# A gated feed-forward block in fp32: seven block products for the first matmul in place of a plain one, and one level instead of two for the second

## Chip, cores and metric

The kernel runs on one core of a Trainium2 chip. The metric is the device time of one execution in microseconds, on the slowest (here the only) core; three runs of the kernel before gave 2157.34, 2160.28 and 2160.47 us. All inputs and outputs are float32.

## The reference

One layer of a decoder: 512 tokens, width 2048. The first half (modulation vectors, an input projection, windowed attention, sparse attention with top-k keys, an output projection) is untouched in its arithmetic. What matters here is the second half:

```python
D_MODEL = 2048; SEQ = 512; D_FF = 5632
def conv_ffn(h, w_up, conv_w, conv_b, w_down):
    u, g = jnp.split(h @ w_up, 2, axis=-1)
    u = causal_depthwise_conv_width_3(u, conv_w) + conv_b
    return (jax.nn.silu(u) * g) @ w_down
...
h = rms_norm(x, norm_ffn[l]) * (1.0 + sc2) + sh2
x = x + g2 * conv_ffn(h, w_up[l], conv_w[l], conv_b[l], w_down[l])
return rms_norm(x, norm_final)
```

`h @ w_up` is (512 x 2048) by (2048 x 11264): the first product. `(...) @ w_down` is (512 x 5632) by (5632 x 2048): the second.

## The kernel before

**Precision.** TensorE (PE) multiplies in fp32r. Each fp32 operand is cut into a high part (a cast on ScalarE, ACT) and a low part (a subtraction on VectorE, DVE): `split` (L155) and `split_to` (L201). A product is three matmuls, high x high, high x low, low x high (`mm3`, L162).

**Slots.** The program is a list of slots. `drive` (L385) goes through it: for slot i it starts the loads of the slots up to 5 ahead (`AHEAD_LOAD`, L28), the cuts of those up to 3 ahead (`AHEAD_SPLIT`, L30), then the matmuls of slot i, then `step` (L307), which lets every started generator go on by one piece, and the slot's `after`. Modulation vectors for later use are computed alongside, paced by the columns PE has been given (`pace`, L290; `mod_gen`, L245; multiply-adds at L216). Dependences are found from the tiles, and a scheduler orders each engine's instructions; `tc.keep_in_program_order` pins some. SP issues the loads, POOL (GpSimd) issues the stores that accumulate in DRAM, and some loads.

**First product.** Row f of 44 stands for 128 of the 5632 features: a unit u of 16 x 128 weight rows and a unit g. `unit_slots` (L368) makes four slots of each unit, 4 contraction tiles x 3 matmuls per slot, the weights stationary and 512 tokens moving (line L53 in the profile). The normalised activations are held as `h2h`, `h2l`. Row f is 96 matmuls of 512 columns. `conv_gen` (L1031) does the convolution, silu and gate; its result stays in SBUF.

**Second product.** Four rows make a group g. While group g runs through the first product, group g - 1 runs through the second: its slots (`down_products`, L1285) are put between those of the first product. A group's (tokens x features) by (features x outputs) product is cut into 2 x 2 blocks and done with seven block products (Strassen's scheme with Winograd's sums) in place of eight: three plain ones (`Product`, L1152; operand sums in `combos`, L1061) and four that are cut once more into 2 x 2 and done with seven again (`Deep`, L1198; `cut_seven`, L1079). Here the activations are stationary and 512 columns of weights move: 72 matmuls in the plain ones and 84 in the deep ones, where a direct product has 192. Weight sums are made on VectorE (L1168, L1171, L1222, L1225). Results go from PSUM (L1194, L1249, L1252) to DRAM, where POOL accumulates them in `total` (`add_up`, L1143). This is done for the first ten groups.

**Close.** The last group (rows 40 to 43) is multiplied directly with 256 tokens moving (`last_slots`, L1329), in two halves of the tokens, 384 matmuls. `join_gen` (L1295) loads `total` on POOL's queue (L1305), transposes it on PE (`cT`) and adds it to the residual `x2`; the final norm and the output stores follow (`finish_half`, L1376). The residual waits in DRAM (`x2d`) from the start of the feed-forward part.

**Memory.** `ring` holds weights in flight and short-lived pairs; `big` holds two tiles of 4 MB, tags b2 and b3, in turn for h1, the mixed attention output mh/ml, and h2. PSUM has eight banks: acc 2, sc 3, tp 2, o 1.

Of the kernel before, what the change touches and what calls it, by code (L numbers as in the profile page):

```python
# [15 lines left out]
P = 128  # L16
# [17 lines left out]
def hybrid_trunk(ctx, tc, xT, cT, wm, bm, nrm, wik, wiq, wi1, sinks, kvn, wuk, wuv, rel, onehot,  # L34
# [26 lines left out]
    ring = ctx.enter_context(tc.tile_pool(name="ring", bufs=1))  # L61
    big = ctx.enter_context(tc.tile_pool(name="big", bufs=1))
    h1h = big.tile([P, KT, T], F32R, tag="b2", name="h1h")
    h1l = big.tile([P, KT, T], F32R, tag="b3", name="h1l")
# [256 lines left out]
    class Raw:  # L321
        def __init__(self, src, name, pool=None):
            self.src, self.name, self.pool, self.t = src.rearrange("p a b -> p (a b)"), name, pool, {}

        def load(self, part):
            if part not in self.t:
                x, name = self.src[:, 512 * part:512 * part + 512], f"{self.name}_{part}"
                if self.pool in env:
                    env["late"] = n = env.get("late", 0) + 1
                    if n < 7:  # L330
                        t = env[self.pool].tile([P, 512], F32, tag="raw", bufs=6, name=name)
                    else:
                        t = ring.tile([P, 512], F32, tag="raw", bufs=RAW, name=name)
                    self.t[part] = t
                    tc.keep_in_program_order(sp.dma_start(t, x))
                else:
                    self.t[part] = load_raw(x, name)
# [12 lines left out]

    class Kept:

        def __init__(self, raw, part, mm, after=None):
            self.raw, self.part, self.mm, self.after, self.w = raw, part, mm, after, None

        def split(self):
            if self.w is None:
                n, part = self.part
                self.w = env["h2h"][:, n], env["h2l"][:, n]
                if self.raw:  # L360
                    self.load()
                    split_to(*self.w, self.raw.t[part])

        def load(self):
            if self.raw:
                self.raw.load(self.part[1])
# [18 lines left out]
    def drive(slots, lo, hi, halves=False, ahead=AHEAD_LOAD):  # L385
        for i in range(lo, hi):
            for j in range(i, min(i + ahead + 1, len(slots))):
                slots[j].load()
            for j in range(i, min(i + AHEAD_SPLIT + 1, len(slots))):
# [590 lines left out]

    def squares(dt, name):
# [14 lines left out]
    def wo_after(dt):  # L996
        def f(ps):
            xk = env["x2"][dt // 4][:, dt % 4]
            with later(-60 if dt == KT - 1 else 0):
                dve.scalar_tensor_tensor(xk, ps, mcol(2, dt), xk, OP.mult, OP.add)  # L1000
                squares(dt, "sq2_")
        return f
# [8 lines left out]

    acts, ugate = {}, {}
    LEAD = 3
# [6 lines left out]
    def g_after(f):  # L1020
        def g(ps):
            start(conv_gen(f, ugate[f], ps))
        return g

    SG = FT // 4 - 1
    total = [[dram.tile([P, 2, T], F32, name=f"total{h}_{dq}") for dq in range(4)] for h in range(2)]
    x2d = [dram.tile([P, 4, T], F32, name=f"x2d{i}") for i in range(4)]
    pair, cuts, keep3, held = {}, {}, {}, {}
    W = P * 2

    def conv_gen(f, ups, gps):  # L1031
        g, k = divmod(f, 4)
        p, half = k % 2, k // 2
        if half == 0:
            pair[g, p] = env["p2"].tile([P, 2, T], F32, tag="u", bufs=2, name=f"cu{g}_{p}")
        u = pair[g, p][:, half]
        act.activation(u, ups, AF.Identity, bias=cb_sb[:, f:f + 1], scale=cw_sb[:, f, 2:3])
        dve.scalar_tensor_tensor(u[:, 1:], ups[:, :T - 1], cw_sb[:, f, 1:2], u[:, 1:], OP.mult, OP.add)
        dve.scalar_tensor_tensor(u[:, 2:], ups[:, :T - 2], cw_sb[:, f, 0:1], u[:, 2:], OP.mult, OP.add)
        act.activation(u, u, AF.Silu)  # L1040
        dve.tensor_tensor(u, gps, u, OP.mult)
        yield
        if g == SG:
            if "pe" in env:
                last_acts(f)
            else:
                env.setdefault("late", []).append(f)
        elif half:
            yield from combos(g, p)

    def last_acts(f):
        g, k = divmod(f, 4)
        fh = env["pe"].tile([P, T], F32R, tag="fh", bufs=4, name=f"fh{f}")
        fl = env["pe"].tile([P, T], F32R, tag="fl", bufs=4, name=f"fl{f}")
        split_to(fh, fl, pair[g, k % 2][:, k // 2])
        acts[f] = fh, fl


    PLAIN, DEEP, TURNS = (0, 2, 3), (1, 4, 5, 6), (1, 5, 4, 6)

    def combos(g, p):  # L1061


        u = pair[g, p].rearrange("p a b -> p (a b)")
        a11, a21, a12, a22 = [u[:, W * i:W * i + W] for i in range(4)]
        if p == 0:
            cuts[g] = [env["pf"].tile([P, 3, 2, W], F32R, tag=f"a{x}", bufs=1, name=f"a{x}{g}") for x in "hl"]
        ah, al = cuts[g]
        k = keep3[g, p] = env["pf"].tile([P, 4, W], F32, tag="op", bufs=2, name=f"op{g}_{p}")
        split_to(ah[:, 0, p], al[:, 0, p], a11)  # L1070
        act.copy(k[:, 0:2], u[:, 2 * W:].rearrange("p (a b) -> p a b", a=2))
        dve.tensor_tensor(k[:, 2], a21, a22, OP.subtract)
        dve.tensor_tensor(a21, a11, a21, OP.subtract)
        yield
        dve.tensor_tensor(a11, k[:, 2], a11, OP.subtract)
        dve.tensor_tensor(k[:, 3], a12, a11, OP.add)
        split_to(ah[:, 1:3, p], al[:, 1:3, p], u[:, :2 * W].rearrange("p (a b) -> p a b", a=2))

    def cut_seven(g, i):  # L1079


        if (g, i) not in cuts:
            ah, al = cuts[g, i] = [env["pd"].tile([P, 7 * P], F32R, tag=f"b{x}", bufs=2, name=f"b{x}{g}_{i}")
                                   for x in "hl"]
            x0, x1 = [keep3[g, p][:, DEEP.index(i)] for p in range(2)]
            split_to(ah[:, :P], al[:, :P], x0[:, :P])
            split_to(ah[:, P:3 * P], al[:, P:3 * P], x1)
            dve.tensor_tensor(x1[:, P:], x0[:, P:], x1[:, P:], OP.subtract)
            dve.tensor_tensor(x0[:, P:], x0[:, :P], x0[:, P:], OP.subtract)
            dve.tensor_tensor(x0[:, :P], x1[:, P:], x0[:, :P], OP.subtract)  # L1090
            dve.tensor_tensor(x1[:, :P], x1[:, :P], x0[:, :P], OP.add)
            split_to(ah[:, 3 * P:5 * P], al[:, 3 * P:5 * P], x0)
            split_to(ah[:, 5 * P:], al[:, 5 * P:], x1)
        return cuts[g, i]

    class Quads:


        BUFS = {0: 2, 1: 1, 2: 2, 3: 2}

        def __init__(self, g):
            self.g, self.b = g, {}

        def load(self, i, c):
            if (i, c) in self.b:
                return
            tag, at = (0, 3) if i == 6 else (i, i)
            t = env["pa"].tile([P, 2, 512], F32, tag=f"rq{tag}", bufs=self.BUFS[tag], name=f"rq{self.g}_{i}_{c}")
            sp.dma_start(t, wdn[self.g, c + 2 * (at % 2)][:, 2 * (at // 2):2 * (at // 2) + 2])
            self.b[i, c] = t  # L1110

    def cut_w(x, n):
        hi_t = env["pd"].tile([P, 2, 512], F32R, tag="dh", bufs=2, name=f"dh{n}")
        lo_t = env["pd"].tile([P, 2, 512], F32R, tag="dl", bufs=2, name=f"dl{n}")
        k = x.shape[1]
        split_to(hi_t[:, :k], lo_t[:, :k], x)
        return [(hi_t[:, i], lo_t[:, i]) for i in range(k)]


    STEPS = {0: ((0, 1), (), 0, ((0, 1, 0),)),  # L1120
             2: ((2, 3), ((1, 3, 1), (0, 3, 3)), 3, ((3, 2, 3),)),
             3: ((), (), 1, ())}

    BLOCK = {1: 2, 4: 3, 5: 0, 6: 6}

    GOES = {1: ((0, 0),), 4: ((1, 0),), 5: ((0, 2), (1, 2)), 6: ((0, 2),)}

    STEPS2 = [((0, 1), (), 0, ((0, 1, 0),)),
              ((2,), ((1, 3, 1), (0, 3, "t")), "t", (("t", 2, 2),)),
              ((3, 6), (), 1, ()),  # L1130
              ((5, 4), (), 0, ())]
    OPERAND = [0, 1, 3, 4, 2, 6, 5]

    SIGN = [1, 1, -1, -1, 1, -1, -1]
# [6 lines left out]
    begun = set()  # L1141

    def add_up(g, to, x):  # L1143
        if id(to) in begun:
            ins = pool.dma_start(to, x, accum_op=OP.add)  # L1145
        else:
            ins = pool.dma_start(to, x)
            begun.add(id(to))
# [472 lines left out]
```

## Time and profile before

| | |
|---|---|
| runs | 2157.34, 2160.28, 2160.47 us; median 2160.28 |
| span of the profiled execution | 2157.9 us (no separate time is given for it; it lies 2.4 us under the median) |
| mean granted TensorE clock | 0.994 |
| busy: PE, VectorE, ScalarE, POOL | 98%, 78%, 55%, 11% |
| moved by DMA | 428.93 MB, mean 199 GB/s |
| feed-forward part up to its closing stage | from 767.3 to 2086.8 us |
| closing stage and end | from 2086.8 to 2157.9 us |

How to read it: PE's busy share counts pipelined matmuls from start to a modelled end, which overlap; the distance between the starts of two of them is what one costs in a full stream. The line of a matmul is L53, that of the helper, so groups go by the names of tiles: `u18ps<-h2h,u18r_2h` is row 18's u unit; `p`, `p_0s` to `p_6s` are plain and deep blocks of the second product (`dh`, `dl` their cut weights, `ah`, `bh` cut activations); `d_0ps` to `d_3ps` the closing stage.

### The profile page before, as it was taken

The numbers are of one execution on the slowest core, as the hardware profiler recorded it, in microseconds if no ns is written. First come the engines' busy times: TensorE is split into PE (matmuls) and PEld (weight loads), VectorE is DVE, ScalarE is ACT, GpSimd is POOL, SyncE is SP. The second block draws the span as 40 slices with busy tenths as digits, with TensorE's granted clock in tenths as the row PEclk, the third lists the DMA queues.
The fourth block names the chain that finished last, engine by engine and source line by source line (L and its number), as shares of the span: only waits on it lengthen the run. The fifth ranks groups of instructions, "written<-read, shape, count | busy, mean of one in ns | idle before, by whom it ended". The sixth has DMA issues, their size and how long they took to land.

```text
span 2157.9 us, 29881 instructions
## 1 busy us (share of the span) xinstructions
PE 2116.7 (98%) x10264; PEld 1721.8 (80%) x10264; DVE 1692.4 (78%) x3005; ACT 1187.4 (55%) x2222; POOL 244.0 (11%) x356
## 2 busy tenths in 40 slices
PE   8999999899999999999999999999999999999997
PEld 4777877787788878888888888888888888888887
DVE  2887899778777775788888878787787877787876
ACT  4324886777722273555555555555555555555554
POOL 0000000111033200101011010111101110111110
PEclk9999999999999999999999999999999999999998
DMA  9783221676598644688888897988778787877772
GB/s 388 266 288 107 58 68 59 198 213 207 174 366 286 228 155 139 199 225 201 221 190 214 219 223 199 223 208 204 189 186 192 193 181 209 174 196 176 168 265 98
DMA packets 160840, 428.93 MB, mean 199 GB/s; under 512 B 18479, under 2 KB 25663, under 8 KB 154544
## 3 DMA queue, kind: packets, MB, share of 16 engines
q1 hardware_dynamic: 118128, 277.09, 38.2%
q0 software_dynamic: 41696, 148.36, 32.4%
q8 instruction: 80, 1.31, 0.2%
q10 hardware_dynamic: 864, 1.57, 0.2%
q14 instruction: 72, 0.59, 0.1%
HBM read 323.41 MB, written 103.55 MB: 198 GB/s over the span
## 4 chain that ended last, share of the span: by engine, by line
PE 85%; DVE 5%; ACT 4%; issue 3%; DMA 2%; POOL 0%; SPq 0%; DVEq 0%; POOLq 0%; ACTq 0%
PE p L53 8%; PE p_0s L53 5%; PE qip L53 4%; PE p_5s L53 1%; PE p_6s L53 1%; PE p_1s L53 1%; PE o L53 1%; PE ckv L53 1%; PE mrow L53 1%; PE scb L53 1%; DVE wk L699 1%; PE mps L53 1%; DVE top L696 1%; DMA ct<-total 1%; DMA mraw<-in_wm_dram 1%
## 5 line engine op out<-in xcount | busy, mean ns | idle before, releaser
L216 DVE SCALAR_TENSOR_TENSOR macc<-mraw,cact,macc 128x512 f32<-128x512 f32 x240 | 179.4, 748 | 12.3 <-DMA mraw<-in_wm_dram 10.3
L203 DVE TENSOR_TENSOR dl<-rq,dh 128x1024 fp32r<-128x1024 f32 x60 | 73.4, 1223 | 45.2 <-ACT dh L202 40.3
L53 PE MATMUL p<-dl,ah 128*128 128x512 f32 x240 | 94.6, 394 | 0.0
L203 DVE TENSOR_TENSOR dl_0s<-rq,dh_0s 128x1024 fp32r<-128x1024 f32 x40 | 49.0, 1226 | 58.0 <-ACT dh_0s L202 57.8
L53 PE MATMUL p<-dh,ah 128*128 128x512 f32 x240 | 94.2, 392 | 0.0
L53 PE MATMUL p<-dh,al 128*128 128x512 f32 x240 | 93.2, 388 | 0.0
L202 ACT CAST dh<-rq 128x1024 fp32r<-128x1024 f32 x60 | 62.7, 1044 | 29.0 <-DVE rq L1168 28.5
L203 DVE TENSOR_TENSOR dl_3s<-rq,dh_3s 128x1024 fp32r<-128x1024 f32 x40 | 48.9, 1223 | 29.4 <-ACT dh_3s L202 29.4
L202 ACT CAST bh<-op 128x256 fp32r<-128x256 f32 (+1 forms) x160 | 58.2, 376 | 22.8 <-DVE op L1090 16.6
L1437 POOL DMA_DIRECT2D mraw<-in_wm_dram x48 | 25.4, 530 | 345.3 <-DVE macc L216 223.9
L1483 POOL DMA_DIRECT2D mraw<-in_wm_dram x96 | 51.4, 537 | 113.0 <-DVE macc L216 73.7
L203 DVE TENSOR_TENSOR bl<-op,bh 128x256 fp32r<-128x256 f32 (+1 forms) x160 | 59.2, 386 | 3.5 <-ACT bh L202 1.5
L1171 DVE TENSOR_TENSOR rq<-rq,rq 128x1024 f32<-128x1024 f32 x40 | 48.8, 1221 | 11.6 <-DMA rq<-in_wdn_dram 11.2
L1145 POOL DMA_DIRECT2D total<-r_5s x40 | 34.8, 1103 | 183.2 <-ACT bh L202 182.9
L53 PEld LDWEIGHTS p<-dh,ah 128*128 128x128 f32 x240 | 45.0, 188 | 10.7 <-ACT v L1194 0.4
L53 PEld LDWEIGHTS p<-dh,al 128*128 128x128 f32 x240 | 45.1, 188 | 10.0
L203 DVE TENSOR_TENSOR dl_2s<-rq,dh_2s 128x1024 fp32r<-128x1024 f32 x40 | 48.9, 1224 | 4.3 <-ACT dh_2s L202 3.7
L53 PEld LDWEIGHTS p<-dl,ah 128*128 128x128 f32 x240 | 45.1, 188 | 8.8
L554 DVE TENSOR_TENSOR qi<-qi,qip 128x512 f32<-128x512 f32 x56 | 38.3, 684 | 14.4 <-PE qip L53 13.7
L1168 DVE TENSOR_TENSOR rq<-rq,rq 128x1024 f32<-128x1024 f32 x40 | 48.9, 1223 | 0.8
L202 ACT CAST dh_2s<-rq 128x1024 fp32r<-128x1024 f32 x40 | 41.9, 1049 | 1.4
L202 ACT CAST dh_3s<-rq 128x1024 fp32r<-128x1024 f32 x40 | 41.6, 1041 | 0.0
(4573 smaller groups left out, 7348.8 us busy)
## 6 DMA issues: line engine op xcount, KB each, us to landing
rq<-in_wdn_dram SPq DMA_DIRECT2D x100, 512.0 KB
mraw<-in_wm_dram SPq DMA_DIRECT2D x32, 1024.0 KB
mraw<-in_wm_dram POOLq DMA_DIRECT2D x48, 512.0 KB, 6.6
mraw<-in_wm_dram POOLq DMA_DIRECT2D x96, 256.0 KB, 6.5
total<-u POOLq DMA_DIRECT2D x40, 512.0 KB, 7.8
total<-r_5s POOLq DMA_DIRECT2D x40, 512.0 KB, 10.9
mraw<-in_wm_dram SPq DMA_DIRECT2D x64, 256.0 KB
total<-e POOLq DMA_DIRECT2D x20, 512.0 KB, 5.7
```

What stands on the lines that cost most here:

```text
L53: return self.to.matmul(out, w, x, **kw)
L202: act.copy(hi_t, full)
L203: dve.tensor_tensor(lo_t, full, hi_t.bitcast(F32), OP.subtract)
L216: tc.keep_in_program_order(dve.scalar_tensor_tensor(acc, t, cact[:, kt:kt + 1], acc, OP.mult, OP.add))
L554: dve.tensor_tensor(qi[i], qi[i], ps, OP.add)
L696: dve.max(top[b][:, r], cur[b])
L699: dve.match_replace(wk[b], top[b][:, r], cur[b], -3e38)
L1145: ins = pool.dma_start(to, x, accum_op=OP.add)
L1168: dve.tensor_tensor(b[z, c], b[x, c], b[y, c], OP.add)
L1171: dve.tensor_tensor(b[z, c], b[x, c], b[y, c], OP.add)
L1437: pool.dma_start(two[0], wm[g, kt // 4][:, kt % 4:kt % 4 + 2])
L1483: pool.dma_start(t, wm[g, kt // 4][:, kt % 4])
```

## The change

1. **First product.** Rows 0 to 2 stay plain. Rows 3 to 43 are done by seven block products per row: u and g are the two block rows on the weight side, the contraction's two halves the block columns, and the tokens' two halves the block columns of the activations. A product is 8 contraction tiles x 3 matmuls of 256 tokens; a row is 7 slots (`Duo`). The sums of the activations' blocks are made once (`t_forms`, `t1_form`), those of the weights for each row on VectorE (`duo_cut`). Three PSUM banks collect the products; they are copied or added to SBUF between products (`Duo.out`). Convolution, silu and gate then work from SBUF.
2. **Activations through DRAM.** Each row's result is stored by ScalarE's queue to `actd` (`store_act`).
3. **Second product afterwards.** Once the first is done, five groups of eight rows are read back (`stage_load`), cut into 2 x 2 blocks and multiplied by one level of seven (`Down`), for the two halves of the output columns in turn: 14 slots of 12 matmuls of 512 columns each. The second level is gone. Block results are copied to SBUF and accumulated in `total` by POOL, 7 stores for each half of a group.
4. **Close.** As before for rows 40 to 43, whose activations are read from `actd`; the quarters come in the order 0, 2, 1, 3, and the loads of `total` start with the closing stage. The signs and the held-back last block are gone.
5. **Memory and queues.** `big` holds eight tiles of a quarter each per use; `ring` moves to the other side and is closed after row 2; its place is taken by `ut`. Cut weights take turns in four buffers that were `x2`'s. The residual is stored to `x2d` piece by piece from ScalarE's queue. Modulation loads beside the first product go through POOL's queue. From the first product by sevens on, loads of raw weights have one buffer for each of the four blocks.

The core of the diff:

```diff
+    def whole(name):
+        return [Pieces([big.tile([P, 4, T], F32R, tag=f"b{'hl'[i]}{j}", name=f"{name}{'hl'[i]}{j}")
+                        for j in range(4)]) for i in range(2)]
+
+    h1h, h1l = whole("h1")
...
+    def store_x2(dt):
+        yield
+        act.dma_start(x2d[dt // 4][:, dt % 4], env["x2"][dt // 4][:, dt % 4])
...
+    ORDER = (1, 2, 6, 5, 7, 3, 4)
+    NP = 3
+    GROUPS = FT // 8
...
+    def cut(x, name):
+        w = env["px0"].tile([P, 2, 1024], F32R, tag=f"x2_{cut_turn[0] % 4}", name=f"w{name}")
+        cut_turn[0] += 1
+        split_to(w[:, 0], w[:, 1], x)
+        return w[:, 0], w[:, 1]
+
+    def conv(f, y, u):
+        act.activation(y, u, AF.Identity, bias=cb_sb[:, f:f + 1], scale=cw_sb[:, f, 2:3])
+        dve.scalar_tensor_tensor(y[:, 1:], u[:, :T - 1], cw_sb[:, f, 1:2], y[:, 1:], OP.mult, OP.add)
+        dve.scalar_tensor_tensor(y[:, 2:], u[:, :T - 2], cw_sb[:, f, 0:1], y[:, 2:], OP.mult, OP.add)
+        act.activation(y, y, AF.Silu)
...
+    def duo_cut(f, pos):
+        a, b, c, d = [duo_raw[f, t] for t in "abcd"]
+        name = f"u{f}_{pos}"
+        if pos == 0:
+            return cut(a, name)
+        if pos == 1:
+            w = cut(b, name)
+            dve.tensor_tensor(a, a, c, OP.subtract)
+            return w
+        if pos == 2:
+            s = duo_raw[f, "s"] = fr_tile("s", f"rs{f}")
+            dve.tensor_tensor(s, d, a, OP.subtract)
+            return cut(s, name)
+        if pos == 3:
+            dve.tensor_tensor(c, c, d, OP.add)
+            w = cut(c, name)
+            duo_load(f + 1, "c")
+            return w
...
+    class Duo:
...
+        def mm(self, w):
+            box, i = self.box, ORDER[self.pos]
+            if i == 1:
+                box["x"] = bank("acc", f"ux{self.f}")[:, :W]
+            elif i == 2:
+                box["z"] = bank("sc", f"uz{self.f}")[:, :W]
+            elif i == 5:
+                box["y"] = bank("tp", f"uy{self.f}")[:, :W]
+            ps = box[{2: "z", 5: "y", 3: "y"}.get(i, "x")]
...
+            for k in range(8):
...
+                pe.matmul(ps, wh, xh, start=new and k == 0, stop=False, **go)
+                pe.matmul(ps, wh, xl, start=False, stop=False, **go)
+                pe.matmul(ps, wl, xh, start=False, stop=k == 7, **go)
...
+            if i == 1:
+                box["u"] = ut.tile([P, T], F32, tag="u", bufs=2, name=f"ut{f}")
+                act.copy(box["u"][:, :W], box["x"])
+            elif i == 2:
+                dve.tensor_tensor(box["u"][:, :W], box["u"][:, :W], box["z"], OP.add)
+            elif i == 6:
+                act.copy(box["u"][:, W:], box["x"])
...
+            elif i == 7:
+                dve.tensor_tensor(box["g"], box["g"], box["x"], OP.add)
+            elif i == 3:
+                dve.tensor_tensor(box["u"][:, W:], box["u"][:, W:], box["y"], OP.add)
+                box["o"] = ut.tile([P, T], F32, tag="y", bufs=3, name=f"y{f}")
+                conv(f, box["o"], box["u"])
...
+    def down_tiles():
+        down_t["stage"] = [place(f"h{k}", f"stage{k}", (P, 4, T)) for k in range(2)]
+        ca, bd = place("l0", "rawca"), place("l1", "rawbd")
...
+    class Down:
...
+            for b, ps in enumerate(box["y" if i in (2, 5, 3) else "x"]):
+                tok = slice(P * b, P * b + P)
+                for k in range(2):
+                    kt = 2 * self.p + k
+                    wh, wl = [x[:, T * k:T * k + T] for x in w]
+                    pe.matmul(ps, ah[:, kt, tok], wh, start=new and kt == 0, stop=False, **go)
+                    pe.matmul(ps, ah[:, kt, tok], wl, start=False, stop=False, **go)
+                    pe.matmul(ps, al[:, kt, tok], wh, start=False, stop=kt == 3, **go)
...
+            e = evac_place().rearrange("p (a b) -> p a b", a=2)
+            for b, ps in enumerate(self.box["y" if i in (2, 5, 3) else "x"]):
+                act.copy(e[:, b], ps)
+            h, dq = {1: (0, 0), 2: (0, 0), 6: (0, 2), 5: (1, 2), 7: (1, 2), 3: (0, 2), 4: (1, 0)}[i]
+            add_up(total[h][dq + c], e)
...
+    for f in range(NP, FT):
+        box = {}
+        slots += [Duo(f, pos, box) for pos in range(7)]
+    marks["down"] = len(slots)
+    for n in range(2 * GROUPS):
+        box = {}
+        slots += [Down(n, pos, p, box) for pos in range(7) for p in range(2)]
...
+    ringc.__exit__(None, None, None)
+    utc = tc.tile_pool(name="ut", bufs=1, side="right", reuse_waits="tile")
+    env["ut"] = utc.__enter__()
+    pace(mod_gen(range(20, 24), raw_mod, 3, env["ut"], o_bank), 28000)
+    drive(slots, marks["duo"], marks["down"] - 3, ahead=3)
+    down_tiles()
+    stage_load(0)
+    for t in "acdb":
+        for p in range(2):
+            dn_load(0, p, t)
+    drive(slots, marks["down"] - 3, marks["down"] - 1, ahead=2)
+    down_tiles2()
+    drive(slots, marks["down"] - 1, marks["down"] + 2)
+    finish_all()
```

More of the change, by code (lines that the diff above doesn't have):

```diff
@@ L327, in load @@
                 x, name = self.src[:, 512 * part:512 * part + 512], f"{self.name}_{part}"
[L328 to L337, printed above, removed]
+                self.t[part] = load_raw(x, name)
     class Slot:
@@ L388, in drive @@
                 slots[j].load()
-            for j in range(i, min(i + AHEAD_SPLIT + 1, len(slots))):
+            for j in range(i, min(i + min(ahead, AHEAD_SPLIT) + 1, len(slots))):
                 slots[j].split()
@@ L1021, in g @@
         def g(ps):
-            start(conv_gen(f, ugate[f], ps))
+            start(plain_conv(f, ugate[f], ps))
         return g
[L1025 to L1045, printed above, removed]
-            else:
-                env.setdefault("late", []).append(f)
-        elif half:
-            yield from combos(g, p)
@@ new lines, in down_tiles2, with raw_place, stage, stage_load @@
+    def down_tiles2():
+        t = place("h2", "rawst")
+        down_t["s"], down_t["spare"] = t[:, 0], t[:, 1]
+        down_t["form"] = place("l2", "af4", dt=F32R)
+        down_t["e"] = [x[:, j] for x in (place("h3", "ev0"), place("l3", "ev1")) for j in range(2)]
+    def raw_place(tag, p, name):
+        return down_t[tag] if p else fr_tile(tag, name)
+    def stage(k):
+        return down_t["stage"][k]
+    def stage_load(g):
+        if g < GROUPS:
+            for k in range(2):
+                sp.dma_start(stage(k), actd[2 * g + k])
@@ L1314, in join_gen, with load @@
+    def join_gen():
+        ct = env["ct"]
+        def load(j):
+            for h in range(2):
+                tc.keep_in_program_order(pool.dma_start(ct[j % 2][h], total[h][LAST[j]]))
+        for j in range(2):
+            load(j)
+        yield
+        for j, dq in enumerate(LAST):
             for i in range(4):
@@ L1530, in hybrid_trunk @@
-    for f in env.pop("late", []):
-        last_acts(f)
-    start(join_gen(len(slots) - 32 - marks["join"]))
-    drive(slots, marks["join"], len(slots), ahead=12)
+    drive(slots, marks["last"] - 14, marks["last"] - 6)
+    last_acts()
+    drive(slots, marks["last"] - 6, marks["last"])
+    t = env["tt"].tile([P, 4, 2, T], F32, tag="t7", name="ct")
+    env["ct"] = [[t[:, 2 * j + h] for h in range(2)] for j in range(2)]
+    t = env["tail"] = env["tt"].tile([P, 8, T], F32, tag="t4", name="tail")
@@ L1534, in hybrid_trunk, with mt @@
+    turn_m = [0]
+    def mt():
+        turn_m[0] += 1
+        return t[:, 2 + turn_m[0] % 4]
+    env["mt"] = mt
+    start(join_gen())
+    drive(slots, marks["last"], len(slots), ahead=12)
     finish_all()
```

606 lines of the change are left out of this document (293 added, 313 removed).

## The prediction

> **What bounds the kernel now.** I read the page first: busy shares, slices, the chain that ended last.
>
> ```profile
> span 2157.9 us, 29881 instructions
> PE 2116.7 (98%) x10264; PEld 1721.8 (80%) x10264; DVE 1692.4 (78%) x3005; ACT 1187.4 (55%) x2222; POOL 244.0 (11%) x356
> ...
> PE 85%; DVE 5%; ACT 4%; issue 3%; DMA 2%; POOL 0%; SPq 0%; DVEq 0%; POOLq 0%; ACTq 0%
> ```
>
> TensorE (PE) is busy 98% of the span and is 85% of the chain. A busy PE need not be an efficient one, so I went on to the windows: the feed-forward part up to its closing stage, 200 us inside it, and for the memory rate an earlier stage of heavy loading.
>
> ```profile
> core 0: us, PE busy (x) PEld busy (x) DVE busy (x) ACT busy (x) POOL busy (x), PEclk, DMA share, GB/s
> 767.30:2086.80 1319.50, 1317.86 (x5817) 1089.06 (x5818) 1042.99 (x1650) 732.35 (x1203) 152.53 (x182) 1.00 0.79 200
> 1000.00:1200.00 200.00, 199.90 (x885) 165.08 (x884) 163.08 (x255) 107.90 (x179) 25.82 (x30) 1.00 0.86 214
> 600.00:700.00 100.00, 100.00 (x454) 83.14 (x453) 80.08 (x126) 28.11 (x46) 35.40 (x66) 1.00 0.94 336
> ```
>
> In 1319.5 us PE stops for 1.6 and its granted clock is 1.00, with VectorE (DVE) at 82% beside it (163.08 of 200). Only fewer PE microseconds can shorten this stage; a heavier VectorE can lengthen it. A matmul's price is the distance between starts, not its busy time, since they are pipelined. The timeline of PE gives it, by the first and last of unbroken runs:
>
> ```profile
> 785.25 0.39 PE L53 MATMUL u0ps<-h2h,u0r_2h 128*128 128x512 f32 x1
> ...
> 793.41 0.39 PE L53 MATMUL u0ps<-h2h,u0r_3h 128*128 128x512 f32 x1
> ...
> 875.06 0.39 PE L53 MATMUL p<-dh,ah 128*128 128x512 f32 x1
> ...
> 877.81 0.39 PE L53 MATMUL g4ps<-h2h,g4r_1h 128*128 128x512 f32 x1
> ...
> 2127.71 0.28 PE L53 MATMUL d_0ps<-fh,h2h 128*128 128x256 f32 x1
> ...
> 2137.79 0.28 PE L53 MATMUL d_0ps<-fh,h2h 128*128 128x256 f32 x1
> ```
>
> First product: 36 matmuls in 8.16 us, 226.7 ns each at 512 columns. Plain blocks of the second: 12 in 2.75 us, 229.2 ns; for its deep blocks I take the first product's price. Closing stage at 256 columns: 84 in 10.08 us, 120.0 ns. So 256 columns cost 106.7 ns and each matmul 13.3 ns besides: halving the width is not halving the price.
>
> Check: the stage has 88 x 48 = 4224 matmuls of the first product, ten groups of 72 plain and 84 deep ones, and 32 small ones at about 0.12: 957.6 + 165.0 + 190.4 + 3.8 = 1316.8 us, of 1319.5 measured. The counting holds.
>
> **The change, part by part.** *First product, rows 3 to 43.* Removed: 41 x 96 = 3936 matmuls at 226.7 ns, 892.3 us. Added: 41 rows x 7 products x 8 x 3 = 6888 at 256 columns and 120.0 ns, 826.6 us. Saved: 65.7 us (one eighth would be 111; the 13.3 ns on twice as many instructions eat the rest).
>
> [...]
>
> *Second product.* Removed: 720 at 229.2 and 840 at 226.7, 355.4 us. Added: 5 groups x 2 halves x 14 slots x 12 = 1680, their operands laid out like the plain blocks', so 229.2 ns: 385.1 us (380.9 at 226.7). Cost 29.7 us. Undoing the second level gives back nearly half of what the first product saves. Net of PE: **-36.0 us**.
>
> *VectorE in the first product.* Now the other engines must fit in a shorter row. PE's row is 168 x 120.0 ns = 20.2 us. VectorE per row: seven low-part subtractions and four combinations of 128x1024, three additions and two multiplications at 256 columns out of PSUM, two convolution steps, and 64 modulation steps shared by 41 rows. By start-to-start:
>
> ```profile
> 1241.52 0.74 DVE L1038 SCALAR_TENSOR_TENSOR cu<-u16ps,cw_sb,cu 128x511 f32<-128x511 f32 x1
> 1242.30 0.75 DVE L1039 SCALAR_TENSOR_TENSOR cu<-u16ps,cw_sb,cu 128x510 f32<-128x510 f32 x1
> ...
> 1254.71 1.22 DVE L1171 TENSOR_TENSOR rq<-rq,rq 128x1024 f32<-128x1024 f32 x1
> 1255.85 1.22 DVE L203 TENSOR_TENSOR dl<-rq,dh 128x1024 fp32r<-128x1024 f32 x1
> 1256.99 0.68 DVE L159 TENSOR_TENSOR u17r_2l<-u17r,u17r_2h 128x512 fp32r<-128x512 f32 x1
> ...
> 2096.01 0.48 DVE L1339 SCALAR_TENSOR_TENSOR x2b<-d_0ps,mod,x2b 128x256 f32<-128x256 f32 x1
> 2096.40 0.48 DVE L1339 SCALAR_TENSOR_TENSOR x2b<-d_1ps,mod,x2b 128x256 f32<-128x256 f32 x1
> ```
>
> 11 x 1.14 + 5 x 0.39 + 2 x 0.78 + 64 x 0.78 / 41 = 12.5 + 2.0 + 1.6 + 1.2 = 17.3 us of 20.2 (a modulation step at the price of a convolution step, of the same form). There is 2.9 us a row to spare, less than anywhere now. What may fill it is waiting, above all a subtraction for ScalarE's (ACT) cast of the same weights:
>
> ```profile
> L203 DVE TENSOR_TENSOR dl<-rq,dh 128x1024 fp32r<-128x1024 f32 x60 | 73.4, 1223 | 45.2 <-ACT dh L202 40.3 <-DMA rq<-in_wdn_dram 4.4 <-PE u8ps L53 0.5
> ...
> L203 DVE TENSOR_TENSOR dl_0s<-rq,dh_0s 128x1024 fp32r<-128x1024 f32 x40 | 49.0, 1226 | 58.0 <-ACT dh_0s L202 57.8
> L203 DVE TENSOR_TENSOR dl_2s<-rq,dh_2s 128x1024 fp32r<-128x1024 f32 x40 | 48.9, 1224 | 4.3 <-ACT dh_2s L202 3.7
> L203 DVE TENSOR_TENSOR dl_3s<-rq,dh_3s 128x1024 fp32r<-128x1024 f32 x40 | 48.9, 1223 | 29.4 <-ACT dh_3s L202 29.4
> ...
> L202 ACT CAST dh<-rq 128x1024 fp32r<-128x1024 f32 x60 | 62.7, 1044 | 29.0 <-DVE rq L1168 28.5
> ```
>
> 136.9 us over 180 cuts is 0.76 us a cut, 5.3 us for seven: more than the 2.9. But today VectorE waits because it is early; when late it finds the casts made, as cuts run three slots (8.6 us) ahead. Unavoidable are the three cuts a row whose input VectorE itself has just made: 3 x 1.04 = 3.1 us, about the room, if nothing is put between. I take 0 (bounds 0 and +98 us: 17.3 + 5.3 - 20.2 = 2.4 a row, 41 rows), by the windows, where PE does not stop beside a VectorE at 82%. ACT has 7 x 1.04, under four for evacuation and convolution, and a store issue per row: about 12 of 20.2. Behind a store that waits for its row stand ACT's next cast and the copy that frees bank x; the store is issued one slot after the row is due, which hides it.
>
> *VectorE in the second product.* A column half is 14 x 12 x 229.2 ns = 38.5 us of PE. VectorE has 22 x 1.14 = 25.1 us, and in the first half of each group eleven more for the activations' forms, 37.6. Full but inside: 2 us in all (0 to 15). Accumulating stores fall from 178 (10 x 18, less 2 kept back) to 70; POOL gains room.
>
> *The changes of stage.* Here the cover is gone: before, the second product ran among the first's slots; now each stage's buffers are the stage before's. Rows for what moves: the landing of the sums' loads, one issue on POOL, and PE's waits at earlier changes of stage.
>
> ```profile
> ct<-total POOLq DMA_DIRECT2D x8, 512.0 KB, 5.9
> ```
> ```profile
> 2059.66 1.19 POOL L1305 DMA_DIRECT2D ct<-total  x1
> ```
> ```profile
> PE wo0ps L53 <- ACT mh L202: 2.4, 1, 2.4
> ...
> PE u0ps L53 <- ACT h2h L197: 1.2, 1, 1.2
> ```
>
> Plain rows to blocks of seven: ring memory is handed over, while the first two products need no new evacuation: 2 us (0 to 5; nearest row the 1.2 of the stage's start). First to second product: 2.1 MB of activations and 4.2 MB of weights can load only when the fourth slot from the end is done, 8.6 us ahead. At 336 GB/s activations and the first block (2.6 MB) take 7.8 us, with about 2 of latency and 2.3 of cutting a stop of 3 or 4; the second block lies seventh in SP's queue, 5.8 MB or 17 us, another 3 or 4: 7 us (2 to 14). Second product to closing stage: the sums' loads queue on POOL behind the last accumulations: 1.2 of evacuation, two to three issues of 1.2, 5.9 to landing, some 10 us, of which the first closing slots hide about 6: 4 us (0 to 8). Front: h1 and mh in pieces can take back part of the 2.4 stop; residual stores go from SP to ACT's queue, 16 instead of 4: -1 (-5 to +2). With the 2 above: **+14 us** (-3 to +44).
>
> **Sum.** 2157.9 - 36.0 + 14 = 2135.9 us. The page gives no time of its own run beside the span; this span lies among the runs (2157.34 to 2160.47), 2.4 under their median, so the forecast is 2138 us.
>
> **Rivals.** *All covers hold*: no stop at any change of stage, 2124 us. For it: 100% busy now; against: buffers of one copy. Chance 0.12. *VectorE sets the row's pace in the first product*: its order is fixed, so it waits for casts or loads with other work behind it, cuts come late, and PE waits each row. The price reaches 98 us; at the middle 49, 2187, slower. It undoes the gain from 22 / 41 = 0.54 us a row. For it: 17.3 of 20.2 and the 0.76 us a cut; against: three slots of lead, and no PE stop at 82% now. Chance 0.20. *Stage changes eat the gain*: 36 us of stops, near 2160, no change; for it the single buffers, against it the sums above. 0.08. *The fixed part shrinks in long runs of 256-wide matmuls*: at half of 226.7, 113.4 ns, 45.5 us less, 2093. [...] 84 in a row without it: 0.02.
>
> **How the numbers follow.** Forecast 0.55, own range 2121 to 2153 (changes of stage at -3 to +29); the rivals 0.12, 0.20, 0.08, 0.02; 0.03 for the unforeseen, some of it slower. Faster 0.55 + 0.12 + 0.02 + 0.01 = 0.70, same 0.08, slower 0.22; 0.2% (4.3 us) is about what a measurement can tell from no change. The range goes from 2114, below the rival without stops, to 2187, the middle of VectorE's rival.
>
> **What would show it.** Right: 256-wide starts 120.0 ns apart in the first product, 7 x 8 x 3 a row, rows of about 20.2 us; second product 229 ns; stops of a few us at three places only. Wrong: PE waits recurring in every row with VectorE's sums or low parts as releaser, VectorE over 90% busy; a gap over 10 us between products, with loads as releaser; or a pitch other than 120.

## The result, and the profile after

The changed kernel takes 2171.33 us (median of 4 runs, 2169.81 to 2173.38), the kernel before in the same comparison 2160.38 (2157.34 to 2161.61): a ratio of 1.0057, 95% interval 1.0043 to 1.0071. It is 11 us slower, where 22 us less were forecast. The profiled execution of the changed kernel took 2173.38 us, its span is 2171.6; the two spans differ by 13.7 us.

The page after, with the lines that answer to those of before (busy shares and the chain that ended last):

```profile
span 2171.6 us, 34457 instructions
PE 2100.9 (97%) x13336; PEld 1836.1 (85%) x13336; DVE 1717.1 (79%) x2522; ACT 1143.7 (53%) x1907; POOL 181.0 (8%) x310
...
PE 68%; DVE 11%; DMA 11%; ACT 7%; issue 3%; SPq 0%; DVEq 0%; POOL 0%; ACTq 0%; POOLq 0%
```

PE has 3072 more, shorter matmuls and 16 us less of busy time, so work did go. But its share of the chain fell from 85 to 68%: the path to the end now runs through loads and through VectorE and ScalarE. The windows of the feed-forward part, in order its three plain rows, the rows by seven and the second product (busy time of each engine, granted clock, DMA share, GB/s):

```profile
776.40:845.10 68.70, 67.52 (x288) 53.91 (x289) 63.82 (x82) 50.58 (x70) 2.14 (x4) 1.00 0.25 81
845.10:1687.30 842.20, 833.99 (x6921) 830.83 (x6920) 682.70 (x798) 384.57 (x490) 32.24 (x60) 1.00 0.43 138
1687.30:2095.40 408.10, 391.43 (x1682) 316.82 (x1682) 326.23 (x291) 253.23 (x327) 56.80 (x69) 0.99 0.88 230
```

The first thing to read is PE's idle time, 8.2 us in the rows by seven and 16.7 in the second product, where the same 1319.5 us of before had 1.6. VectorE is at 81% in the rows by seven (682.70 of 842.20, 16.7 us a row): by its sum it is not the bound. What PE waited for, from the end of attention to the closing stage (PE's tile, the releaser, us in total, times, the longest):

```profile
PE p L53 <- DVE wd L216: 8.7, 7, 3.6
PE tpb L57 <- ACT etb L824: 6.3, 2, 5.9
PE p L53 <- ACT ev L1331: 5.2, 5, 1.8
PE ux L53 <- DVE gt L1151: 4.6, 6, 1.1
PE d_2ps L53 <- ACT ev L1331: 3.7, 1, 3.7
PE p L53 <- ACT wd L215: 2.0, 2, 1.4
PE ux L53 <- ACT ut L1142: 1.9, 3, 0.9
PE uy L53 <- ACT gt L1149: 1.5, 2, 0.9
```

The names tell two things. More than half of these 33.9 us are waits for a *copy out of a bank* by ScalarE (`etb`, `ev`, `ut`, `gt` of L1149: 18.6 us), a short operation (0.37 us for one `gt`); what can hold it back is something ahead of it in its engine's queue, which the experiments test. And `tpb` is in attention, which the change should not touch.

The matmuls' pitch, by the first and last start of unbroken runs in PE's timeline: 24 of a slot by seven, then 34 of the output projection in the front, and last 12 of the same projection in the kernel before.

```profile
1001.82 0.28 PE L53 MATMUL uy<-h2h,wu 128*128 128x256 f32 x1
...
1004.70 3.04 PE L53 MATMUL ux<-t_up,wu 128*128 128x256 f32 x24
```
```profile
700.20 0.40 PE L53 MATMUL wo10ps<-ml,wo10r_0h 128*128 128x512 f32 x1
...
708.13 0.40 PE L53 MATMUL wo10ps<-mh,wo10r_3l 128*128 128x512 f32 x1
```
```profile
699.80 0.39 PE L53 MATMUL wo10ps<-mh,wo10r_3l 128*128 128x512 f32 x1
...
702.52 0.39 PE L53 MATMUL wo11ps<-mh,wo11r_0l 128*128 128x512 f32 x1
```

2.88 us / 24 is the forecast 120.0 ns. But 7.93 / 34 is 233.2 ns, where the same kind of matmul took 2.72 / 12, 226.7 ns, before: the 512-wide matmuls with weights from the ring are some 6 ns slower. So the spans compare as follows. "Stops" are here the sums of what start-to-start distances exceed the pitch of the same matmuls by, where that is over 60 ns; they hold waits and matmuls at half the clock.

| stage | before, us | after, us | forecast, us |
|---|---|---|---|
| front, to the first u0 matmul | 767.3 | 776.4 | 766.3 |
| plain rows | - | 68.7 = 288 x 233.3 ns + stops 1.6 | 65.3 |
| rows by seven | - | 842.2 = 826.6 + stops 12.7 + modulation 3.2 | 826.6 + 2 for the change of stage |
| second product | - | 408.1 = 1680 x 227.0 ns (381.3) + stops 26.8 | 385.1 + 2 + 7 |
| feed-forward in all | 1319.5 | 1319.1 | 1294.5 |
| closing stage, end | 71.1 | 76.1 | 75.1 |

(The forecast for the feed-forward part was 1319.5 - 36.0 + 2 + 2 + 7. Its three rows add up to 1288.0; the other 6.5 are the prediction's 3.8 for small matmuls of the modulation and the 2.7 that the kernel before had beside its counted matmuls.) PE's own sums hold, the second product's even 4 us better, since its matmuls take 227.0 ns and not the 229.2 of the forecast. All that is missing lies in stops, in the front, and in 1.9 us of slower plain rows. Some 1.7 us of the stops among the rows by seven are no waits but gaps of about 0.1 us each; a kernel below in which the view lists no wait of PE there has as many.

### The profile page after: what moved, and what is told of

It is laid out like the page before. It is cut to its first block, busy times and chain, and to the rows that moved or that the text cites. A ratio compares the mean times of both kernels' runs of the same rounds, so it can differ in the third digit from the quotient of the medians.

```text
span 2171.6 us, 34457 instructions
## 1 busy us (share of the span) xinstructions
PE 2100.9 (97%) x13336; PEld 1836.1 (85%) x13336; DVE 1717.1 (79%) x2522; ACT 1143.7 (53%) x1907; POOL 181.0 (8%) x310
## 4 chain that ended last, share of the span: by engine, by line
PE 68%; DVE 11%; DMA 11%; ACT 7%; issue 3%; SPq 0%; DVEq 0%; POOL 0%; ACTq 0%; POOLq 0%
PE ux L53 15%; PE p L53 11%; PE uy L53 6%; PE uz L53 4%; PE qip L53 4%; DVE wu L216 3%; DMA ra<-in_wup_dram 2%; DMA rd<-in_wup_dram 2%; PE o L53 1%; DMA qd<-in_wdn_dram 1%; DMA rawbd<-in_wdn_dram 1%; PE ckv L53 1%; DVE wd L216 1%; ACT wu L215 1%; PE mrow L53 1%
## 5 line engine op out<-in xcount | busy, mean ns | idle before, releaser
L53 PE MATMUL p<-wd,af 128*128 128x512 f32 x1680 | 391.7, 394 | 16.7 <-DVE wd L216 8.7
L53 PEld LDWEIGHTS p<-wd,af 128*128 128x128 f32 x1680 | 316.8, 190 | 91.2 <-DVE wd L216 13.4
L53 PE MATMUL ux<-t_up,wu 128*128 128x256 f32 x2952 | 375.8, 284 | 6.6 <-DVE gt L1151 4.6
L53 PEld LDWEIGHTS ux<-t_up,wu 128*128 128x128 f32 x2952 | 362.7, 192 | 9.1 <-DVE gt L1151 6.0
L53 PE MATMUL uy<-h2h,wu 128*128 128x256 f32 x1312 | 249.8, 283 | 1.6 <-ACT gt L1149 1.5
L53 PEld LDWEIGHTS uy<-h2h,wu 128*128 128x128 f32 x1312 | 210.5, 192 | 2.2 <-ACT gt L1149 2.2
L53 PE MATMUL uy<-h2l,wu 128*128 128x256 f32 x656 | 185.6, 283 | 0.0
L53 PEld LDWEIGHTS uy<-h2l,wu 128*128 128x128 f32 x656 | 125.9, 192 | 0.0
L53 PE MATMUL ux<-h2h,wu 128*128 128x256 f32 x656 | 124.8, 283 | 0.0
L53 PE MATMUL uz<-h2h,wu 128*128 128x256 f32 x656 | 124.7, 283 | 0.0
```

The source lines that it names most:

```text
L53: return self.to.matmul(out, w, x, **kw)
```

## The experiments

Three theories came from these views. **A**: the 6 ns come from where the two operands of a matmul lie in memory. **C**: the stops are ScalarE's in-order queue: a cast that waits for a load blocks the copies that free PE's banks. **The rival** of the prediction: VectorE (or ScalarE) has too much work. Of 10 kernels, the times of some vary by several us from run to run, with the stops; where a single stop is asked for, the stage in the trace decides.

### Where the operands lie

One unused tile of 32 bytes a partition ahead of the activations, in the kernel before and in the kernel after. All instructions and their order stay; the activations move by 32 bytes against the ring's weights.

```diff
+    big.tile([P, 8], F32, tag="pad", name="pad")
     h1h = big.tile([P, KT, T], F32R, tag="b2", name="h1h")
```

> The kernel before with one unused tile of 32 bytes a partition ahead of the activations' tile, nothing else: every instruction and its order stay, only the activations and what lies behind them move by 32 bytes, while the weights of the stacked columns stay where they are. Theory A (the distance between the addresses of a matmul's two operands sets its pitch at 512 columns: 226.7 ns where both lie 32 bytes past a multiple of 64, as in the kernel before; 233.3 where one does and the other doesn't, as in the kernel after): the 4224 matmuls of the first product go from 226.7 to about 233.3 ns, 28 us more; the attention's and output projection's 2160 add some 9 and the plain blocks of the second product up to 3; in all near 2200 us. Theory B (weights at the upper end of the memory, or activations in four pieces, make the 233.3): no change, 226.7 ns and 2160 us.

Measured: 2196.14 us against 2159.21, ratio 1.0173 (1.0156 to 1.0190). 36 starts of the first product in this kernel, 8.41 us, 233.6 ns each (233.3 over all unbroken u and g matmuls):

```profile
793.41 0.40 PE L53 MATMUL u0ps<-h2h,u0r_2h 128*128 128x512 f32 x1
...
801.82 0.40 PE L53 MATMUL u0ps<-h2h,u0r_3h 128*128 128x512 f32 x1
```

> The kernel after with the same unused tile of 32 bytes ahead of the activations' pieces; instructions and order unchanged. Theory A: the 512-wide matmuls whose weights come from the ring go back from 233.3 to about 226.7 ns, 10 us less in the front and 2 in the plain rows: near 2159.5 us, front 766. The products by sevens, whose two operands move together, stay at 120.0 and 227.0 ns. Theory B: no change, 2171.

Measured: 2173.27 us, ratio to before 1.0067 (1.0044 to 1.0090): no gain in time. In the trace the front went from 776.4 to 770.8 us and the plain rows from 68.7 to 67.5, but the rows by seven from 842.2 to 849.2 (stops 19.5 instead of 12.7) and the closing stage from 76.1 to 78.3. The 512-wide pitch went to 229 ns, not to 226.7. With the addresses that the allocator gave, as bytes past a multiple of 256 (activations / ring weights), the mean pitches of the first product's u and g matmuls in all these kernels read:

| kernel | activations | weights | pitch, ns |
|---|---|---|---|
| before | 32 | 32 | 226.7 |
| before, tile of 32 | 64 | 32 | 233.3 |
| after | 0 | 224 | 233.3 |
| after, tile of 32 | 32 | 224 | 229.0 |
| after, tile of 224 (below) | 224 | 224 | 227.1 |

Theory B is refuted: neither the upper end of memory nor the pieces matter, an unused tile alone makes and unmakes the cost. A's simple form (only the remainder by 64 counts) is too simple: 32 and 224 have the same remainder and cost 2.3 ns. That also explains a row of the prediction: the plain blocks of the second product before stood at 32 and 224 and took 229.2 ns. With the tile of 32 they stood at 64 and 224 and took 233.2, while the deep blocks, whose operands moved together (64 and 64), stayed at 227.0. So in these kernels the pitch goes with the distance between the two: 226.7 to 227.1 ns at none, 229.0 and 229.2 at 64 bytes (counted around 256), 233.2 and 233.3 at 32 and 96. Why equal distances are cheapest stays open.

### Two copies of the raw blocks, and more work for VectorE

ScalarE's waits for loads among the rows by seven, in the kernel after:

```profile
ACT wu L215 <- DMA ra<-in_wup_dram: 35.2, 14, 4.0
ACT wu L215 <- DMA rb<-in_wup_dram: 11.4, 5, 3.3
```

A row has one buffer for each raw block. Block a is loaded when its last cut is done, and cut again three slots later, after 8.6 us; around 1160 us the issue stands at 1159.43 and the cast starts at 1166.26, having waited 3.97 us with the copies `gt` behind it.

```diff
-        t = duo_raw[f, tag] = fr_tile(tag, f"r{tag}{f}")
+        own = (f - NP) % 2
+        t = duo_raw[f, tag] = (env["ut"].tile([P, 1024], F32, tag=f"r{tag}", ...) if own
+                               else fr_tile(tag, f"r{tag}{f}"))
...
-            duo_load(f + 1, "c")
+            for t in "acbd":
+                duo_load(f + 1, t)
```

> The kernel after with the four raw weight blocks of a row by sevens in two copies (odd rows take theirs from memory that is free in this stage) and loaded together at the row's fourth cut. Theory C (the 12.7 us of stops in the first product come from raw blocks that land too late: ScalarE's cast waits for the load and the copies of finished sums wait behind it): ScalarE's waits for the loads of ra and rb, 46.6 us now, go; PE's stops in the first product fall from 12.7 to under 3 us, the time to about 2161 us. Theory D (VectorE's or ScalarE's own work is too much for a row of 20.2 us): stops stay within 2 us of 12.7, the time at 2170 or 2171.

Measured: 2165.46 us, 1.0032 (1.0020 to 1.0044). The rows by seven took 831.5 us instead of 842.2, with 1.7 us of stops; ScalarE's waits for `ra` and `rb` are gone, and the view lists no wait of PE there. The time fell by 6 us; in the profiled execution the second product and the closing stage were 4 us longer than in the kernel after. C holds.

> The kernel with two copies of the raw blocks, and two more 128x1024 subtractions on VectorE a row (2.28 us, their result is not used), so 19.6 us of work by the prediction's count in a row of 20.2. Theory K (VectorE's 2.9 us of room a row are real, and it was never what stopped PE): first product within 4 us of 831.5 us. Rival L (VectorE has no more to give: waits for casts fill its room): up to 2.28 us a row, 94 us in all; with half of the room gone, 40.

```diff
         w = cut(d, name)
+        for _ in range(2):
+            dve.tensor_tensor(duo_raw[f, "s"], d, c, OP.subtract)
```

Measured: 2167.77 us, 1.0050 (1.0031 to 1.0068). The windows of the rows by seven, first with two copies, then with VectorE's extra work:

```profile
843.20:1674.70 831.50, 831.50 (x6921) 830.38 (x6920) 682.04 (x798) 383.03 (x490) 32.29 (x60) 1.00 0.44 140
```
```profile
845.80:1677.10 831.30, 831.30 (x6922) 830.39 (x6921) 769.17 (x878) 381.98 (x489) 32.18 (x60) 1.00 0.43 139
```

VectorE at 769.17 of 831.30, 93%, and PE does not stop for a moment. The extra work is 87 us, 2.1 us a row, so at least that much of the predicted room of 2.9 us was real; the rival that VectorE sets the pace of these rows is refuted.

### The front

The 5.9 us stop stands at 562.9 us. ScalarE's timeline just before it (start, us, operation, and in brackets its idle time before):

```profile
553.53 0.19 ACT L803 ACTIVATION_READ_ACCUMULATOR sb<-sb,nmb 128x1 f32 x1
560.53 0.62 ACT L215 CAST mh<-mxr 128x512 fp32r<-128x512 f32 x1 [6.82 <-DMA mxr<-mixd]
561.05 0.50 ACT L803 ACTIVATE sb<-sb,nmb 128x256 f32<-128x256 f32 x1
```

The cast of a reloaded attention output stands in the middle of a softmax. Before, `mh` was one tile that came free only after the last projection; now its pieces come free one by one, and the scheduler placed the cast earlier, ahead of its load's landing. A one-column copy from the last heads' keys holds it back:

```diff
                 if kt == 8:
+                    act.copy(mh[:, kt][:, 0:1], kb[7][:, 0][:, 0:1])
                 mix_in(kt)
```

> The kernel after with one tiny copy on ScalarE that holds back the casts of the reloaded attention outputs until the last heads' keys are cast. Theory E (the 5.9 us stop at the end of attention, and the half clock that follows it, come from a cast that was put ahead of the softmax in ScalarE's queue and waits there 6.8 us for its load): the stop goes, the clock stays whole at 565 us, the front is 7 to 9 us shorter, about 2163 us. Rival F (the softmax is late for another reason, or the wait moves to VectorE's queue, where the low parts stand): front within 2 us of 776, 2170 us.

Measured: 2174.97 us, 1.0076 (1.0053 to 1.0099): no gain. In the trace the stop fell to 2.6 us (before had one of 2.4 near there), and the front went from 776.4 to 771.9, 4.5 us of the 7 to 9 expected. (In the five kernels with an unchanged front it lies between 774.5 and 777.1 us.) The rest of this run gave it back in longer stops later (second product 31.1 us instead of 26.8, rows by seven 15.6 instead of 12.7). E is shown for the place, not for the time.

### The change to the second product, and its end

> The kernel after with the first group's activations loaded some 40 slots earlier into memory that is free in the first product, so that at the change from the first product to the second only weights load and two of the seven operand forms can be made ahead. Theory G (the stops of 9 us between 1687 and 1708 us come from loads that start late and from VectorE's queue of 22 operations behind them): they fall to 5 us or less and the half clock at 1699 goes; about 2166 us. Rival H (VectorE's work of the change of stage is the bound wherever the loads stand): within 2 us of 9.

```diff
+    env["st"] = [env["ut"].tile([P, 4, T], F32, tag=f"st{k}", name=f"st{k}") for k in range(2)]
+    stage_load(0)
+    drive(slots, marks["down"] - 40, marks["down"] - 3, ahead=3)
     down_tiles()
-    stage_load(0)
```

(The pool `ut`, which holds these two tiles, is closed 13 slots later.)

Measured: 2174.19 us, 1.0084 (1.0067 to 1.0101). At the place, stops fell from 9.1 to 4.1 us; but the rows by seven took 3.9 us more than in the kernel after (ScalarE's waits for `ra` and `rb` 63.5 us instead of 46.6, stops 16.5) and other stops filled the rest. G holds at the place, and nothing of it reached the end. What PE met there in the kernel after was VectorE's queue more than a load: in VectorE's timeline, and in ScalarE's for the last line, the longest stop (3.58 us, to 1699.08) ends with the low part `wd<-rawbd`.

```profile
1686.92 1.23 DVE L216 TENSOR_TENSOR af<-stage,af 128x1024 fp32r<-128x1024 f32 x1 [0.89 <-ACT af L215]
...
1697.81 1.22 DVE L216 TENSOR_TENSOR wd<-rawbd,wd 128x1024 fp32r<-128x1024 f32 x1
```
```profile
1693.68 1.04 ACT L215 CAST wd<-rawbd 128x1024 fp32r<-128x1024 f32 x1
```

ScalarE's cast of that block was done at 1694.7, 3.1 us earlier. VectorE came to it late: from 1686.92 to 1704.9 it works without a break, on the activations' sums and cuts and on the weights'.

The end of the second product in the kernel after, by ScalarE's waits from 2040 to 2100 us:

```profile
ACT kept L215 <- DMA wd<-in_wdn_dram: 13.2, 3, 5.9
ACT wd L215 <- DMA rawbd<-in_wdn_dram: 7.4, 1, 7.4
ACT kept L215 <- DMA total<-ev: 4.1, 1, 4.1
```

The casts of the closing stage's weights, `kept`, come when their loads have only begun, and one of them waits until a sum has been stored from the place it is to fill; the copies `ev` stand behind.

> The kernel after with the end of the second product relieved: the first two raw blocks of the kept weights get memory of their own and load 14 slots ahead, the last four rows' activations load into the stage's place instead of one of the four buffers of cut weights, and the last two kept pieces lie in buffers of cut weights instead of in the place of the evacuated sums. No operation is added or dropped. Theory I (the stops of 12 us from 2062 us on and the closing stage's 3.9 are ScalarE's casts waiting for loads and for the sums' stores, with the evacuations behind them): ScalarE's 13.2 us of waits for the kept weights' loads fall below 3, PE's stops from 2062 us to the closing stage's end to about 4 us, the half clock at 2088 and 2101 goes; about 2160 us. Rival J (the accumulating stores set the end): no change beyond 3 us.

```diff
-        raw = env["px0"].tile([P, 4, T], F32, tag=f"x2_{cut_turn[0] % 4}", name="lastr")
+        raw = down_t["stage"][0]
...
+            if n < 2:
+                t = env["kr"].tile([P, 1024], F32, tag=f"kr{n}", name=f"wd{n}")
+            else:
+                t = fr_tile("acsdb"[(n - 2) % 5], f"wd{n}")
...
+        if q not in kept_t and q > 5:
+            kept_t[q] = env["px0"].tile([P, 4, 512], F32R, ...)
```

(The edit also loads the kept blocks one further ahead and cuts the last activations two slots earlier.)

Measured: 2164.37 us, 1.0025 (1.0013 to 1.0038). The windows of the second product's last part, from 2055 us to its end, in the kernel after and then here:

```profile
2055.00:2095.40 40.40, 34.02 (x130) 25.69 (x129) 21.75 (x25) 22.21 (x36) 5.57 (x7) 0.92 0.90 218
```
```profile
2055.00:2089.50 34.50, 34.38 (x152) 28.16 (x152) 23.95 (x28) 23.95 (x37) 5.14 (x6) 1.00 0.73 173
```

PE's 6.4 us of idle time there are gone, and so is the half clock there (0.92 to 1.00); in the closing stage the granted clock was 0.91, where the kernel after had 0.92. ScalarE's waits for the kept loads fell from 13.2 to 6.6 us only, and the closing stage stayed at 76.3: its 3.7 us for `ev` became 1.8 for `ev` and 2.7 for the sums' load. Theory I holds for the second product's end, not for the closing stage.

### All of it together

> The kernel after with everything that the theories call for: an unused tile of 224 bytes so that the ring's weights and the activations lie at the same distance from a multiple of 256, the casts of the reloaded attention outputs held back, the raw blocks a and b of the first product in three buffers instead of two, the first group's activations loaded early, and the relieved end. By the theories: the front 10 to 15 us shorter, plain rows 2, first product 10, the change to the second product 4 to 9, its end and the closing stage 10 to 14; from 2171 to between 2121 and 2135 us, about where the prediction's sum lay. If the theories miss what holds PE up: not under 2150.

(To make room, the modulation's raw weights have three buffers beside the first product instead of four.)

Measured: 2142.36 us, 0.9927 (0.9906 to 0.9948): faster than before, but 7 us above the expected range. Most of the stops that were left lay in the second product, 17.6 us, with VectorE's cuts as releaser; VectorE's wait for raw block d stood at 46.0 us there and ScalarE's for b at 45.1, the same single buffer once more.

> The last kernel, and for the second product a third buffer beside those of the raw blocks b and d (one for each half), so that d of the next column half loads two positions earlier and b one. Theory M (the stops that are left inside the second product, nearly all 12 us of them between 1785 and 1983 us with VectorE's cut as releaser, come from b and d landing late, ScalarE and VectorE waiting 45 and 46 us for them): these waits fall to a quarter, the second product's stops from 17.6 to about 7 us, the time from 2142 to about 2131 us. Rival N (VectorE's 323 us and the stores at a DMA share of 0.87 are the bound there): stops stay within 3 us of 17.6, the time at 2140 or more.

```diff
+        spot = ("d", "b", "x")[(2 * (n - 1) + (tag == "b")) % 3] if tag in "bd" and n else tag
+        if spot == "x":
+            t = env["xr"].tile([P, 1024], F32, tag=f"xr{p}", name=name)
+        else:
+            t = raw_place(spot, p, name)
...
             dn_load(n + 1, p, "a")
+            if n:
+                dn_load(n + 1, p, "d")
```

(The first two blocks of the closing stage's weights give up their own memory here and load into the place of d.)

Measured: 2132.28 us (2130.27 to 2134.38), ratio 0.9878 (0.9863 to 0.9893): 26.5 us, 1.2%, faster than the kernel before, and M as expected: 7.7 us of stops, VectorE's waits for d at 1.8 us and none of ScalarE's for b in the view. The windows of its four stages from the first u0 matmul on:

```profile
767.10:834.10 67.00, 65.81 (x289) 53.95 (x290) 63.23 (x82) 50.35 (x70) 1.06 (x2) 1.00 0.26 75
834.10:1671.60 837.50, 833.23 (x6921) 830.84 (x6920) 688.21 (x802) 387.92 (x493) 33.27 (x62) 1.00 0.46 142
1671.60:2060.30 388.70, 383.90 (x1683) 316.14 (x1682) 325.35 (x292) 255.25 (x327) 56.49 (x69) 1.00 0.90 236
2060.30:2132.60 72.30, 58.06 (x473) 56.10 (x471) 45.88 (x93) 30.03 (x70) 5.12 (x9) 0.93 0.41 129
```

The second product went from 408.1 to 388.7 us with the DMA share still at 0.90 and VectorE's work the same: neither was its bound.

> The same kernel without the unused tile of 224 bytes: every instruction and its order the same, only the addresses differ. Theory A (the distance of the two operands sets the pitch): 512-wide matmuls with the ring's weights at 233.3 ns instead of 226.7, some 10 us in the front and 2 in the plain rows: 12 us longer than the kernel with the tile. Rival (stops elsewhere swallow it, as in the kernel after): within 4 us of it.

Measured: 2138.20 us, 5.9 us more than with the tile of 224 bytes, half of what was expected. The front was 4.4 us longer and the plain rows 3.3 (1.8 of it pitch), while the second product's stops happened to be 3.9 shorter. Of the 10 us expected in the front, only the output projection's came: its starts add up to 184.0 us instead of 179.7. Those of the attention's 768 matmuls with weights from the ring (`qa`, `qb`) add up to 198.7 and 198.8. That the slower matmuls of attention fell into time in which PE waits for the softmax anyway is likely, but was not tried.

## Why the prediction was wrong, point by point

The step that failed is the one on covers, in the words of the prediction: "I take 0 (bounds 0 and +98 us...)" for the first product, "Full but inside: 2 us in all" for the second, and "-1 (-5 to +2)" for the front. By its own terms, the last column with the last kernel:

| term | forecast, us | kernel after | all covers mended |
|---|---|---|---|
| first product, PE | -65.7 | -65.7 (pitch 120.0) | -65.7 |
| second product, PE | +29.7 | +25.9 (381.3 - 355.4) | +25.6 |
| stops among the rows by seven, with the change of stage | 2 | 12.7 | 7.9 |
| stops in the second product, with its change of stage | 2 + 7 | 26.8 | 7.7 |
| closing stage | +4 | +5.0 | +1.2 |
| front | -1 | +9.1 | -0.2 |
| plain rows, pitch | 0 | +1.9 | +0.1 |
| sum | -22.0 | +15.7 | -23.4 |
| difference of the spans | | +13.7 | -25.3 |

*Right:* the counting, the pitch of 120.0 ns and what it makes of the halved width; VectorE's room, as far as it was tried; the mechanism of the change itself. With the covers in place the span is 2132.6, where the forecast span was 2135.9; that kernel has buffers which the one forecast for has not. (The sums are 2 us over the measured differences: of the 2.7 us that before had beside its counted matmuls, part is gone.) The net PE gain was there from the start, 39.8 us; the stops and the front took more than it.

*First product.* The prediction asked whether VectorE fits in the shorter row. It does, with 93% too. What did not fit is a load: single raw blocks, reloaded after their last cut, have three slots (8.6 us), and SP's load (6.8 us for the one issued at 1159.43) plus ScalarE's queue took nearly all of it. PE stopped in 13 places of 41 rows. The rival of VectorE's pace had "waits for casts or loads with other work behind it" in its text and so named half of the mechanism, but on the wrong engine, and with a middle price of 49 us where 10.7 are shown.

*Second product.* The 7 us for the first change of stage were near (9.1), but the path was another: the prediction let PE wait for two loads and their cuts (its 2 us of latency were an estimate; in the kernel before, a load of 512 KB of sums issued at 2097.35 landed after 3.87 us, 2.3 more than 512 KB take at 336 GB/s), and the longest stop came from VectorE's queue behind the activations. Not priced were the loads of b and d within each half (5.4 us in the middle), and that the closing stage's weights are cut among the last slots (12.3 us at the end, some 3 of them matmuls at half clock). "Full but inside" looked at VectorE's sum again, and not at what its operands wait for. The 229.2 ns were taken over from the plain blocks; with both operands at the same distance they became 227.0, which was 3.8 us less and not foreseen.

*Closing stage.* The +4 us came close to the measured +5.0 by luck. The prediction let PE wait for the loads of the sums; these held it for 0.8 us (`ct<-total`). What held it for 3.7 was a last copy `ev`, which stood behind a cast of `kept` that waited 4.1 us for a sum's store, and a stretch at half clock followed.

*Front.* The -1 was made of the pieces, which were to take back part of a stop, and of the residual's stores. Two effects were left out: moving the ring and cutting the activations into pieces changed addresses, and so the pitch, and changed when pieces come free, and so the order on ScalarE. Together they gave 9.1 us where the bounds were -5 and +2; putting the stop right gave 4.5 back, the addresses some 4.4.

*Rivals.* Nearest to what happened came "stage changes eat the gain" (0.08, 36 us of stops near 2160), though only some 26 of about 45 us lay at changes of stage (9.1 and 12.3 us, and 5.0 in the closing stage). "All covers hold" (2124) is what the last kernel approaches. Of the signs that the prediction named, 120.0 ns held and a row of 20.5 us nearly; "stops of a few us at three places only" did not: there were 13 places among the rows by seven alone.

What stays open: how much each of the stops cost in time by itself. They vary by several us from run to run (the rows by seven between 12.7 and 19.5 us in kernels with the same buffers there), and what one edit took away, others partly filled. In the last kernel PE still waits 4.1 us among the rows by seven, for the copies `ut`; the kernel with two copies of all four raw blocks had no such wait.

## What to carry to other kernels

When a stage gets shorter, check the loads before the sums: for each buffer, the time from its last read to its next use against the load's round trip (here 8.6 us against 6.8), and then what stands behind the waiting cast in its engine's queue. A copy that frees a bank was a bad neighbour for a cast that waits for a load: `gt` stood behind a wait of 3.97 us, and without such waits the rows by seven took 831.5 us instead of 842.2. And when an edit moves tiles, print the addresses of both matmul operands before and after: equal distances from a multiple of 256 gave 226.7 to 227.1 ns here, unequal ones 229.0 to 233.3.

## What the runs showed of the hardware

- *Pitch by address.* 226.7 to 233.3 ns for the same fp32r matmul of 512 columns, by 32 bytes of one operand's address; 36.9 us on the whole kernel before (2196.14 against 2159.21).
- *Half clock after short stops.* The matmuls after the 3.58 us stop of the kernel after, and after one of 1.87 us in the first kernel with all covers; below each, the window that follows:

```profile
1699.08 6.90 PE L53 MATMUL p<-wd,af 128*128 128x512 f32 x23 [3.58 <-DVE wd L216]
```
```profile
1698.90:1702.30 3.40, 3.22 (x8) 2.60 (x9) 3.40 (x6) 1.22 (x2) 0.00 (x0) 0.53 0.42 125
```
```profile
1862.71 7.58 PE L53 MATMUL p<-wd,af 128*128 128x512 f32 x25 [1.87 <-DVE wd L217]
```
```profile
1863.30:1866.70 3.40, 3.40 (x10) 2.63 (x9) 3.40 (x4) 0.00 (x0) 1.73 (x2) 0.50 1.02 180
```

  At a granted clock near 0.5 (0.53 and 0.50 in these windows), 3.4 us hold 8 matmuls of 427 ns instead of 15 of 227: 1.6 us more, after the stop of 1.87 us nearly as much again. Not every such stop has it: none followed the 1.83 us before 2064.5 in the kernel after. Where the matmul stream went on, the slow stretches in the traces of the kernels before and after last 3.4 or 6.8 us (in the kernel after 1698.7 to 1702.1 and 2087.8 to 2094.6, for two). The shorter of the two stops, 1.87 us, came right after 13 matmuls in 3.11 us.
